# MLP engines bound to source order, and two of four weight-quarter sums made by an accumulating DMA

## The chip, the cores and the metric

One Trainium2 chip, of which this kernel uses one core. The metric is the device time of one execution in microseconds, as the median of several runs. The engines of the core are PE (TensorE, matrix products), DVE (VectorE), ACT (ScalarE), POOL (GpSimd) and SP (SyncE), which here only starts transfers. Each engine runs its own instructions in their order in the program and waits on semaphores for the others.

## What is computed

Two layers of a diffusion backbone over 512 latent tokens and 256 context tokens of width 1024. Each layer has adaLN modulation, an RMSNorm, a token mixer (retention, latent attention, pooling) with a gated residual, then a second norm and the MLP with its gated residual. The change concerns the MLP and what is woven into it:

```python
def rmsnorm(x, g):
    return x * lax.rsqrt(jnp.mean(x * x, axis=-1, keepdims=True) + EPS) * g

def sq_relu_mlp(h, w1, w2):
    return jnp.square(jax.nn.relu(h @ w1)) @ w2

for l in range(DEPTH):
    mod_x = silu(c) @ w_ada[l] + b_ada[l]          # six vectors: sh1, sc1, g1, sh2, sc2, g2
    ...
    x = x + g1 * ox
    x = x + g2 * sq_relu_mlp(modulate(rmsnorm(x, norm_mlp[l]), sh2, sc2), w_ff1[l], w_ff2[l])
    if not last:
        ...
        h = h + cg2 * sq_relu_mlp(modulate(rmsnorm(h, norm_mlp[l]), csh2, csc2), w_ff1[l], w_ff2[l])
return rmsnorm(x, norm_final)
```

Everything is float32. Layer 0 runs the MLP on latent and context tokens, layer 1 on latent tokens alone.

## The kernel before

**Products.** A float32 value is held as a high and a low part; one product of 128 x 128 weights is three matrix multiplications (`mm3`, all of them on line L206). Weights come as raw tiles by DMA and are split by `split_piece`: ACT copies the high part (L214), DVE subtracts it for the low part (L223). The results are the `wt` tiles, six of them.

**The MLP** (`layer_ff`) goes in chunks, eight in layer 0 and four in layer 1. A chunk of layer 0 has four *up* products (tile `f`, from `h`; 48 multiplications of 384 columns each), each evacuated by `evac`: ACT applies ReLU and the square (L1409, L1411), then high and low parts and differences (`T`, L1363, L1364; `act`) are made on ACT and DVE in turn. The first two ups of the first chunk run as one pair (`up_two`), over three groups of tokens, with the norm's last statistics (`ssum`) beside them. Then come two blocks of seven products (A11, S1, A12, S4, S3, S2, A22) of a fast 2 x 2 multiplication scheme, in which two quarters of a weight are first added: S1 = A21 + A22, S3 = A11 + A21, S2 = S1 + A11, S4 = S2 + A12. The four sums are DVE additions (`sum`, L250). A product's PSUM buffer is read out by additions into `V` (L1363) and by *gates*, which add it, scaled, to the residual stream `x` (L1453); there are three such PSUM buffers. The last chunk of each layer is plain: no sums.

**adaLN rows.** While layer 0's MLP runs, the rest of the modulation is computed: some rows as PE products (`ada` from `rows`), the others as dot products on DVE (L474, `dot` and `rows`), one or two for a row. Each row's weights are a 256 KB load (L239) into one of three `rows` tiles. Fourteen such row tasks are merged among the up products of each chunk but the last; the first chunk has eight more, and four ada tasks.

**What sets the order.** `emit` runs the tasks in their order; it loads weight units three ahead on SP's queue (a unit of the blocks is 1 MB, two loads of 512 KB on L231, of four raw tiles in all), splits pieces four ahead, and loads rows up to eight tasks ahead as row tiles become free. A scheduler then reorders each engine's own instructions.

Of the kernel before, what the change touches and what calls it, by code (L numbers as in the profile page):

```python
# [8 lines left out]
F32 = mybir.dt.float32  # L9
F32R = mybir.dt.float32r  # L10
AF = mybir.ActivationFunctionType
ALU = mybir.AluOpType
# [3 lines left out]
P = 128  # L16
# [12 lines left out]
UW = 1024  # L29
# [30 lines left out]
AL = 3  # L60
AU = 4
RA = 8
N_RR = 3
N_DP = 22
N_T = 7
AK = 6
# [10 lines left out]
class Task:  # L77


    def __init__(self, cost, fn, units=()):  # L80
        self.cost, self.fn, self.units = cost, fn, units
# [9 lines left out]
class Unit:  # L91

    def __init__(self, ap, w, kind=None, queue=None):
        self.ap, self.w, self.kind, self.queue = ap, w, kind, queue
        self.raw, self.sums = None, {}
        if kind == "st":
            n = 8  # L100
        elif kind is None:
            n = 1 if w <= OW else -(-w // 512)
        else:
            n = 1
        self.size = w if n == 1 else 512
        self.pieces = [Piece(self, i) for i in range(n)]
        self.nr = {None: 1, "st": 2}.get(kind, 0)
# [19 lines left out]
A11, A12, A22, A21, S1, S2, S3, S4 = range(8)  # L127
# [16 lines left out]
        out.append(t)  # L144


class Net:
    def __init__(self, nc, tc, es, a):
        self.nc, self.tc, self.a = nc, tc, a
        self.n = 0  # L150
        pool = lambda name, bufs, **k: es.enter_context(tc.tile_pool(name=name, bufs=bufs, **k))
        self.cst = pool("cst", 1)
        self.sm = pool("sm", 4)
        self.wr = pool("wr", N_R)
        self.wh = pool("wh", N_W)
        self.tp = pool("tp", N_T)
        self.dp = pool("dp", N_DP)
        self.ps = self.half = None
        self.es = es
        self.psum(3, 2)  # L160
        self.raw, self.hl, self.used = {}, {}, {}
# [64 lines left out]
    def load_unit(self, u):  # L226
        q = u.queue(self.nc) if u.queue else self.nc.sync
        if u.kind == "st":
            u.raw = [self.wr.tile([P, UW], F32, tag="r", name=self.nm("raw")) for _ in range(2)]
            for i in range(2):  # L230
                q.dma_start(u.raw[i], u.ap[:, i * 1024:i * 1024 + 1024])  # L231
            return
        if u.kind == "dp":
            r = self.dp.tile([P, UW], F32, tag="d", name=self.nm("raw"))
        elif u.kind == "wr":
            r = self.wr.tile([P, RW], F32, tag="rr", name=self.nm("rows"), bufs=N_RR)
        else:
            r = self.wr.tile([P, UW], F32, tag="r", name=self.nm("raw"))
        q.dma_start(r[:, :u.w], u.ap)  # L239
        u.raw = r  # L240

    def quarter(self, u, i):

        if i < 4:
            return u.raw[i // 2][:, i % 2 * 512:i % 2 * 512 + 512]
        if i not in u.sums:
            a, b = {S1: (A21, A22), S2: (S1, A11), S3: (A11, A21), S4: (S2, A12)}[i]
            a, b = self.quarter(u, a), self.quarter(u, b)
            t = u.sums[i] = self.tmp("sum")[:, 0:512]
            self.nc.vector.tensor_tensor(t, a, b, op=ALU.add)  # L250
        return u.sums[i]
# [12 lines left out]
    def emit(self, tasks):  # L264
# [37 lines left out]
        for i, t in enumerate(tasks):  # L302
            while ahead < len(rows) and first[rows[ahead]] <= i + RA and sum(end[v] >= i for v in rows[max(0, ahead - 8):ahead]) < N_RR:
                self.load_unit(rows[ahead].unit)
# [1013 lines left out]
    def layer_ff(self, l, whole, groups):  # L1318
# [5 lines left out]
        nc, a = self.nc, self.a  # L1324
        last = l == DEPTH - 1
        w = NL if last else T
# [3 lines left out]
        n_chunk, n_blk = 16 // CP, 4 // MP  # L1330
        halves = [[(0, 256, 0)], [(256, 256, 0)]] if last else [[(0, 384, 0)], [(384, 128, 0), (512, 256, 1)]]
        H = lambda k: self.h[k]
        out = []
# [15 lines left out]
            self.mark = self.lo(lo, src, hi)  # L1349

        def begin():
            n = per * 2 // 4
            t = [self.d("V", F32).rearrange("p a t -> p (a t)") for _ in range(-(-3 // n))]
            for i, name in enumerate("U57"):
                st[name] = [t[i // n][:, (i % n * 4 + j) * hw:(i % n * 4 + j + 1) * hw] for j in range(4)]
                st[name, "all"] = t[i // n][:, i % n * 4 * hw:(i % n + 1) * 4 * hw].rearrange("p (j t) -> p j t", t=hw)
# [75 lines left out]
        def up_two(us):  # L1432

            ps = [self.A("f1") for _ in us]
            for o, n, _ in groups:
                for k in range(NK):
                    s = slice(k * P, (k + 1) * P)
                    for i, u in enumerate(us):
                        self.mm3(ps[i][:, o:o + n], u[:, 0, s], u[:, 1, s],
                                 H(k)[:, 0, o:o + n], H(k)[:, 1, o:o + n], k == 0, k == NK - 1)  # L1440
            for i in range(2):
                for half in range(2):
                    o = half * hw
                    evac(0, i, half, [(ps[i][:, o:o + hw], o, hw)])
# [47 lines left out]
        def finish(j):  # L1492

            U, v5, v7 = (st[n][j] for n in "U57")
            add(v7, v7, U)
            gate(2 * j + 1, 0, v7, True)
            add(U, U, v5)
            add(v7, v7, v5)
            gate(2 * j, 1, U)
            gate(2 * j + 1, 1, v7, True)  # L1500
# [24 lines left out]
        for c in range(n_chunk):  # L1525
            us = [Unit(a["w_ff1"][l, 2 * CP * c + m], 1024) for m in range(2 * CP)]
            m0, ups = 0, []
            cost = self.lin_cost(NK, [(0, hw)] * 2)
            if c == 0:
                m0 = 2  # L1530
                ups.append(Task(0, begin))
                ups.append(Task(2 * cost, lambda us=us: up_two(us[:2]), tuple(us[:2])))
            for m in range(m0, 2 * CP):
                ups.append(Task(cost, lambda c=c, m=m, u=us[m]: up(c, m, u), (us[m],)))
            if c == 0:
                ups.append(Task(0, negate))
            if c == n_chunk - 1:
                ups = merge(ups, [Task(1, lambda j=j: finish(j)) for j in range(4)])
            extra = self.extra.pop(("ff1", l), []) if c == 0 else []
            share = -(-len(spread) // max(n_chunk - 1 - c, 1))  # L1540
            extra, spread = extra + spread[:share], spread[share:]
            out += merge(ups, extra)
            blocks = [Unit(a["w_ff2"][l, c * n_blk + blk], 2048, "st") for blk in range(n_blk)]
            if c < n_chunk - 1:
                for blk in range(n_blk):
                    out += block(c, blk, blocks[blk])
        out.append(Task(0, self.stat_start))
        for blk in range(n_blk - 1):
            out += plain_tasks(c, blocks[blk], blk, whole)
        late = []  # L1550
# [80 lines left out]
def _quarters(w, pairs):  # L1631


    n = 4 // pairs
    t = w.reshape(16 // n, n, 2, P, 4 // pairs, pairs, 2, P)
    t = t.transpose(0, 4, 3, 6, 2, 5, 1, 7).reshape(16, P, 2, 2, 512)
    return np.stack([t[:, :, 0, 0], t[:, :, 0, 1], t[:, :, 1, 1], t[:, :, 1, 0]], axis=2).reshape(16, P, 2048)


def _rope_tables(length, dim):  # L1640
# [101 lines left out]
```

## Time and profile before

| | |
|---|---|
| median of 3 runs | 1658.19 us (1657.01 to 1659.78) |
| the profiled execution | 1657.6 us, its span 1655.8 us |
| PE busy | 1552.9 us, 94% of the span |
| DVE busy | 1183.5 us, 71% |
| ACT busy | 802.4 us, 48% |
| POOL busy | 38.2 us, 2% |
| chain that ended last | PE 84%, DVE 10%, DMA 3%, ACT 3% |

The span is the time from the first to the last instruction of the profiled execution. The chain that ended last is followed back from the last instruction to whatever released each step; it names the engine that sets the end. The idle time shown beside a group of instructions is that of its engine just before them, with the instruction or transfer that ended it.

### The profile page before, as it was taken

The numbers are of one execution on the slowest core, as the hardware profiler recorded it, in microseconds if no ns is written. First come the engines' busy times: TensorE is split into PE (matmuls) and PEld (weight loads), VectorE is DVE, ScalarE is ACT, GpSimd is POOL, SyncE is SP. The second block draws the span as 40 slices with busy tenths as digits, with TensorE's granted clock in tenths as the row PEclk, the third lists the DMA queues.
The fourth block names the chain that finished last, engine by engine and source line by source line (L and its number), as shares of the span: only waits on it lengthen the run. The fifth ranks groups of instructions, "written<-read, shape, count | busy, mean of one in ns | idle before, by whom it ended". The sixth has DMA issues, their size and how long they took to land.

```text
span 1655.8 us, 24510 instructions
## 1 busy us (share of the span) xinstructions
PE 1552.9 (94%) x9100; PEld 1351.4 (82%) x9100; DVE 1183.5 (71%) x2564; ACT 802.4 (48%) x1635; POOL 38.2 (2%) x78
## 2 busy tenths in 40 slices
PE   5999999999869898999999998998999999999997
PEld 2898577878659798899988997976888788888976
DVE  5665756877787979779787948678556785867834
ACT  4425477545334343434434345267764655445443
POOL 0010000000000000000000000101000000000000
PEclk8999999999879899999999999999999999999999
DMA  9352545652433234332432231723433223242321
GB/s 368 112 150 64 148 103 127 193 188 84 128 114 109 96 108 133 116 121 96 131 112 84 88 109 63 208 80 86 101 103 121 77 89 103 71 121 73 119 89 51
DMA packets 69095, 191.98 MB, mean 116 GB/s; under 512 B 8944, under 2 KB 11504, under 8 KB 68976
## 3 DMA queue, kind: packets, MB, share of 16 engines
q1 hardware_dynamic: 65584, 180.18, 34.7%
q0 software_dynamic: 2816, 9.70, 2.6%
q8 instruction: 72, 1.18, 0.3%
q10 hardware_dynamic: 576, 0.52, 0.1%
q14 instruction: 47, 0.39, 0.1%
HBM read 159.97 MB, written 10.49 MB: 103 GB/s over the span
## 4 chain that ended last, share of the span: by engine, by line
PE 84%; DVE 10%; DMA 3%; ACT 3%; issue 1%; SPq 0%; DVEq 0%; ACTq 0%
PE f L206 48%; PE A L206 10%; PE sc L206 4%; PE oe L206 3%; PE pv L206 3%; PE res L206 3%; PE rv L206 2%; PE pT L1031 2%; PE ada L206 2%; DVE act L223 1%; DVE rows L474 1%; PE ro L206 1%; DMA rows<-w_adaT 1%; PE q L206 1%; DVE dot L474 1%; DMA raw<-w_ada 1%
## 5 line engine op out<-in xcount | busy, mean ns | idle before, releaser
L206 PE MATMUL f<-h,wt 128*128 128x384 f32 (+2 forms) x2400 | 466.9, 355 | 10.3 <-ACT b L1409 7.7
L206 PE MATMUL f<-act,wt 128*128 128x256 f32 (+2 forms) x2664 | 436.1, 324 | 41.2 <-DVE x L1453 15.3
L206 PEld LDWEIGHTS f<-h,wt 128*128 128x128 f32 x2400 | 419.9, 191 | 54.3 <-ACT b L1409 14.2
L206 PEld LDWEIGHTS f<-act,wt 128*128 128x128 f32 x2664 | 411.5, 195 | 64.1 <-DVE x L1453 17.2
L223 DVE TENSOR_TENSOR wt<-raw,wt 128x512 fp32r<-128x512 f32 x326 | 222.0, 687 | 150.5 <-ACT wt L214 148.1
L214 ACT ACTIVATE wt<-raw 128x512 fp32r<-128x512 f32 x326 | 201.4, 627 | 228.1 <-PE f L206 124.9
L206 PE MATMUL A<-h,wt 128*128 128x512 f32 (+2 forms) x864 | 171.9, 357 | 1.0 <-ACT h L554 0.5
L206 PEld LDWEIGHTS A<-h,wt 128*128 128x128 f32 x864 | 143.0, 190 | 27.5 <-ACT h L554 2.8
L214 ACT ACTIVATE wt<-sum 128x512 fp32r<-128x512 f32 x104 | 63.0, 628 | 154.2 <-DVE sum L250 143.0
L1409 ACT ACTIVATE b<-f 128x384 f32<-128x384 f32 (+2 forms) x98 | 50.5, 518 | 149.5 <-PE f L206 135.0
L206 PE MATMUL sc<-k,q 96*128 96x512 f32 (+1 forms) x384 | 85.5, 350 | 2.6 <-ACT p L1013 1.9
L474 DVE SCALAR_TENSOR_TENSOR rows<-rows,sbc 128x512 f32<-128x512 f32 x128 | 84.4, 686 | 1.9 <-DMA rows<-w_adaT 1.4
L206 PEld LDWEIGHTS sc<-k,q 96*128 96x128 f32 x384 | 62.8, 188 | 20.4 <-issue 5.5
L1363 DVE TENSOR_TENSOR V<-V,f 128x768 f32<-128x768 f32 (+1 forms) x86 | 62.5, 726 | 21.6 <-PE f L206 21.4
L223 DVE TENSOR_TENSOR wt<-sum,wt 128x512 fp32r<-128x512 f32 x104 | 70.6, 686 | 7.5 <-ACT wt L214 7.3
L1453 DVE SCALAR_TENSOR_TENSOR x<-f,mod,x 128x256 f32<-128x256 f32 (+2 forms) x148 | 68.9, 503 | 6.5 <-PE f L206 4.7
L1012 DVE TENSOR_REDUCE st<-sc 128x1 f32<-128x768 f32 x64 | 60.7, 953 | 15.1 <-PE sc L206 14.7
L1032 ACT ACTIVATE pT<-pT 128x384 f32<-128x384 f32 x128 | 56.5, 491 | 22.4 <-PE pT L1031 22.0
L214 ACT ACTIVATE act<-T 128x384 fp32r<-128x384 f32 (+1 forms) x104 | 47.6, 472 | 38.9 <-DVE T L1364 19.5
L223 DVE TENSOR_TENSOR act<-b,act 128x384 fp32r<-128x384 f32 (+2 forms) x94 | 47.5, 515 | 25.0 <-ACT act L214 24.9
L206 PE MATMUL res<-mix,wt 128*128 128x256 f32 (+1 forms) x384 | 59.1, 313 | 2.3 <-DVE om L1052 1.9
L1013 ACT ACTIVATE p<-sc,st 128x768 f32<-128x768 f32 x64 | 57.8, 905 | 5.6 <-DVE st L1012 4.4
(244 smaller groups left out, 1849.6 us busy)
## 6 DMA issues: line engine op xcount, KB each, us to landing
raw<-w_ff SPq DMA_DIRECT2D x128, 512.0 KB, 3.6
rows<-w_adaT SPq DMA_DIRECT2D x128, 256.0 KB, 3.0
raw<-w_in SPq DMA_DIRECT2D x22, 512.0 KB, 4.1
raw<-w_ada SPq DMA_DIRECT2D x16, 512.0 KB, 10.9
rows<-w_ada SPq DMA_DIRECT2D x32, 256.0 KB, 3.1
raw<-w_out SPq DMA_DIRECT2D x16, 512.0 KB, 3.7
x<-xd SPq DMA_DIRECT2D x6, 768.0 KB, 6.8
x<-xT SPq DMA_DIRECT2D x4, 768.0 KB, 6.5
```

Of the source, the lines that this page charges most:

```text
L206: self.nc.tensor.matmul(out, l, r, start=start, stop=stop)
L214: self.nc.scalar.activation(out, src, AF.Copy, **k)
L223: return self.nc.vector.tensor_tensor(out, src, hi.bitcast(F32), op=ALU.subtract)
L474: nc.vector.scalar_tensor_tensor(out, w, 1.0, self.sbc[:, v, half], op0=ALU.mult, op1=ALU.mult, accum_out=acc[:, v, i, j:j + 1])
L1012: nc.vector.tensor_reduce(st[:, 0:1], ps, axis=AX, op=ALU.max, negate=True)
L1013: nc.scalar.activation(p, ps, AF.Exp, bias=st[:, 0:1], accum_out=st[:, 1:2])
L1031: nc.tensor.transpose(ps[:, kt, :], p[:, (k0 + kt) * P:(k0 + kt + 1) * P], self.ident)
L1032: nc.scalar.activation(s["pT", h, qt // 2][:, k0:k0 + 3, c], ps, AF.Copy)
L1363: add = lambda x, y, z, op=ALU.add: nc.vector.tensor_tensor(x, y, z, op=op)
L1409: nc.scalar.activation(b[:, at:at + n], ps, AF.Relu)
L1453: self.mark = nc.vector.scalar_tensor_tensor(x, ps[:, at - o:at - o + n], g[:, cond:cond + 1], x, op0=ALU.mult, op1=ALU.add)
```

## The change

1. Every instruction that PE, DVE and ACT get between `begin` (ahead of the first up) and `end` (behind the last up of the last chunk) is bound behind the one before it on the same engine, by two wrappers (`Ordered`, `Engines`). The scheduler can no longer reorder them. Transfers are not bound. In the listings below these instructions have the wrapper's line, L164.
2. The quarters of a weight of the blocks are stored as A21, A22, A11, A12. A unit's first raw tile (`sums`) is loaded with A21 twice (L265), the second with A11 and A12 (L266), a third of half the size with A22 (L267), of which there are two. Then GpSimd issues a DMA that adds A22 and A11 to the `sums` tile (L269), which makes it S1 and S3. DVE still adds S2 and S4. The plain chunk's units load A21 without the accumulation.
3. The `rows` tiles become two of three, and the memory set aside for GpSimd's transfers becomes 2048 of 4096.

```diff
-N_RR = 3
+N_RR = 2
...
+class Ordered:
...
+    def __getattr__(self, name):
+        f = getattr(self.engine, name)
+        if name == "dma_start":
+            return f
+        if not self.net.strict:
+            self.last = None
+            return f
+
+        def call(*args, **kw):
+            with self.net.tc.issue_after(self.last.ins) if self.last else nullcontext():
+                self.last = f(*args, **kw)
+            return self.last
+
+        return call
...
-            u.raw = [self.wr.tile([P, UW], F32, tag="r", name=self.nm("raw")) for _ in range(2)]
-            for i in range(2):
-                q.dma_start(u.raw[i], u.ap[:, i * 1024:i * 1024 + 1024])
+            u.raw = [self.wr.tile([P, UW], F32, tag="r", name=self.nm(n)) for n in ("sums", "raw")]
+            u.raw.append(self.wr.tile([P, 512], F32, tag="rh", name=self.nm("raw"), bufs=2))
+            r = u.raw[0].rearrange("p (a c) -> p a c", a=2)
+            if u.plain:
+                q.dma_start(r[:, 0, :], u.ap[:, 0:512])
+            else:
+                q.dma_start(r, u.ap[:, None, 0:512].to_broadcast([P, 2, 512]))
+            q.dma_start(u.raw[1], u.ap[:, 1024:2048])
+            q.dma_start(u.raw[2], u.ap[:, 512:1024])
+            if not u.plain:
+                self.nc.gpsimd.dma_start(u.raw[0], u.ap[:, 512:1536], accum_op=ALU.add)
...
-        if i < 4:
-            return u.raw[i // 2][:, i % 2 * 512:i % 2 * 512 + 512]
+        if i not in (S2, S4):
+            t, o = {A21: (0, 0), S1: (0, 0), S3: (0, 1), A11: (1, 0), A12: (1, 1), A22: (2, 0)}[i]
+            return u.raw[t][:, o * 512:o * 512 + 512]
         if i not in u.sums:
-            a, b = {S1: (A21, A22), S2: (S1, A11), S3: (A11, A21), S4: (S2, A12)}[i]
+            a, b = {S2: (S1, A11), S4: (S2, A12)}[i]
...
         def begin():
+            self.strict = True
...
+        def end():
+            self.strict = False
+            self.stat_start()
+
+        out.append(Task(0, end))
...
-    nc = _bacc.Bacc("TRN2", target_bir_lowering=False, num_devices=1, dynamic_dma_scratch_size=4096)
+    nc = _bacc.Bacc("TRN2", target_bir_lowering=False, num_devices=1, dynamic_dma_scratch_size=2048)
```

PE at the start of layer 0's MLP, before: `res` is the mixer's last projection, `f_846` and `f_847` the first two ups, `ssum` a norm statistic, `ada` the modulation's rows.

```order
L206 MATMUL res_4221<-mix_3386,wt_3861 128x256 x3
L206 MATMUL res_4221<-mix_3768,wt_3861 128x256 x3
L206 MATMUL f_846_4342<-h_763_4024,wt_3932 128x256 x3
L206 MATMUL f_846_4342<-h_764_4025,wt_3932 128x256 x3
L206 MATMUL f_846_4342<-h_765_4026,wt_3932 128x256 x3
...
L206 MATMUL f_846_4342<-h_763_4024,wt_3932 128x256 x3
L206 MATMUL ssum_4245<-ss_3787,one 128x256
L206 MATMUL ada_4303<-rows_4266,sc 32x512
L206 MATMUL ada_4303<-rows_4268,sc 32x512
L206 MATMUL f_847_4343<-h_763_4024,wt_4178 128x256 x3
```

The same place after.

```order
L236 MATMUL res_4224<-mix_3768,wt_3861 128x256 x3
L236 MATMUL ssum_4248<-ss_3787,one 128x256
L164 MATMUL ada_4304<-rows_4269,sc 32x512
L236 MATMUL ssum_4248<-sq_4238,one 128x256
L164 MATMUL ada_4304<-rows_4302,sc 32x512
L164 MATMUL ada_4304<-rows_4314,sc 32x512
L164 MATMUL ada_4304<-rows_4319,sc 32x512
L164 MATMUL f_846_4343<-h_763_4024,wt_3932 128x256 x3
L164 MATMUL f_847_4344<-h_763_4024,wt_4178 128x256 x3
```

The first pair of ups moved from ahead of the last `ssum` to behind it and behind four `ada` products, of which before two stand among the ups.

DVE in a late chunk of layer 0, before, around the evacuation of the second up (`b`, `T`, `act`): the `rows` instructions are dot products, `wt` the low part of a weight.

```order
L474 SCALAR_TENSOR_TENSOR rows_7596,acc_7665<-rows_7596,sbc 128x512
L223 TENSOR_TENSOR act_7713<-b_7710,act_7713 128x384
L223 TENSOR_TENSOR wt_7765<-raw_7570,wt_7765 128x512
L1363 TENSOR_TENSOR T_7742<-b_7710,b_7629 128x384
L1364 SCALAR_TENSOR_TENSOR T_7661<-T_7661,b_7710 128x384
L223 TENSOR_TENSOR act_7713<-b_7710,act_7713 128x384
L223 TENSOR_TENSOR act_7746<-T_7742,act_7746 128x384
L223 TENSOR_TENSOR act_7746<-T_7661,act_7746 128x384
L1364 SCALAR_TENSOR_TENSOR T_7742<-T_7661,b_7710 128x384
L250 TENSOR_TENSOR sum_7768<-raw_7571 128x512
L223 TENSOR_TENSOR act_7753<-T_7742,act_7753 128x384
L474 SCALAR_TENSOR_TENSOR rows_7667,acc_7665<-rows_7667,sbc 128x512
```

The same place after.

```order
L164 TENSOR_TENSOR wt_7669<-raw_7522,wt_7669 128x512
L164 TENSOR_TENSOR act_7707<-b_7704,act_7707 128x384 x2
L164 TENSOR_TENSOR T_7736<-b_7704,b_7620 128x384
L164 TENSOR_TENSOR act_7740<-T_7736,act_7740 128x384
L164 SCALAR_TENSOR_TENSOR T_7652<-T_7652,b_7704 128x384
L164 TENSOR_TENSOR act_7740<-T_7652,act_7740 128x384
L164 SCALAR_TENSOR_TENSOR T_7736<-T_7652,b_7704 128x384
L164 TENSOR_TENSOR act_7747<-T_7736,act_7747 128x384
L164 SCALAR_TENSOR_TENSOR rows_7661,acc_7656<-rows_7661,sbc 128x512
L164 SCALAR_TENSOR_TENSOR rows_7664,acc_7656<-rows_7664,sbc 128x512
L164 SCALAR_TENSOR_TENSOR rows_7751,acc_7656<-rows_7751,sbc 128x512
L164 TENSOR_TENSOR wt_7759<-raw_7559,wt_7759 128x512
```

The evacuation is in one piece now, `T` and `act` in turn, with the split of the next weight and the dots behind all of it; the sum S1 is gone.

SP, the loads of the first chunk's rows, before, with the engines that each load waits for.

```order
L239 DMA rows_4301<-w_adaT 128x512 [waits DMAHW2_49,PE_49]
L239 DMA rows_4306<-w_adaT 128x512 [waits DMAHW3_49,PE_49]
L231 DMA raw_4528<-w_ff 128x1024 [waits DMAHW4_49,DVE_49,Activation_49]
L239 DMA rows_4308<-w_ada 128x512 [waits DMAHW5_49,DVE_49]
L239 DMA rows_4313<-w_ada 128x512 [waits DMAHW6_49,DVE_49]
L239 DMA rows_4318<-w_adaT 128x512 [waits DMAHW7_49,DMAHW5_49,PE_49]
L239 DMA rows_4322<-w_adaT 128x512 [waits DMAHW0_49,DVE_49]
L231 DMA raw_4529<-w_ff 128x1024 [waits DMAHW1_49,DVE_49,Activation_49]
```

The same place after.

```order
L277 DMA rows_4302<-w_ada 128x512 [waits DMAHW3_49,PE_49]
L277 DMA rows_4307<-w_adaT 128x512 [waits DMAHW4_49,DMAHW3_49,PE_49]
L277 DMA rows_4309<-w_adaT 128x512 [waits DMAHW5_49,DVE_49]
L277 DMA rows_4314<-w_ada 128x512 [waits DMAHW6_49,DVE_49]
L277 DMA rows_4319<-w_ada 128x512 [waits DMAHW7_49,DVE_49]
L277 DMA rows_4323<-w_adaT 128x512 [waits DMAHW6_49,DMAHW0_49,PE_49]
L277 DMA rows_4325<-w_adaT 128x512 [waits DMAHW7_49,DMAHW1_49,PE_49]
```

With two tiles, each load from the third on waits for PE's product or DVE's dots on an earlier row, alternately.

## Rows read from the trace of the kernel before

**Rows 1.** The page, part 1: busy us of each engine, its share of the span.

```profile
PE 1552.9 (94%) x9100; PEld 1351.4 (82%) x9100; DVE 1183.5 (71%) x2564; ACT 802.4 (48%) x1635; POOL 38.2 (2%) x78
```

**Rows 2.** Busy time by window: span, then PE, PEld, DVE, ACT, POOL, clock, DMA.

```profile
405.40:512.00 106.60, 86.49 (x437) 73.55 (x438) 85.95 (x214) 40.80 (x82) 0.00 (x0) 0.86 0.37 115
512.00:587.90 75.90, 68.02 (x362) 65.01 (x361) 63.51 (x145) 27.74 (x52) 0.00 (x0) 0.93 0.32 102
...
657.20:726.10 68.90, 65.05 (x361) 64.32 (x361) 54.85 (x114) 28.21 (x52) 0.00 (x0) 0.98 0.37 116
...
1376.90:1466.10 89.20, 87.64 (x531) 77.45 (x530) 65.07 (x136) 44.94 (x88) 0.00 (x0) 0.98 0.33 96
```

**Rows 3.** Timeline of PE, start of layer 0's MLP (start, us, instruction, [idle before]).

```profile
405.39 6.25 PE L206 MATMUL f<-h,wt 128*128 128x256 f32 x51 [0.16 <-DVE x L1243]
...
414.15 13.95 PE L206 MATMUL f<-h,wt 128*128 128x256 f32 x103
428.03 1.04 PE L206 MATMUL ada<-rows,sc 128*32 128x512 f32 x2
```

**Rows 4.** Timeline of PE, the fourth chunk of layer 0.

```profile
657.20 29.91 PE L206 MATMUL f<-h,wt 128*128 128x384 f32 x168
...
688.89 4.40 PE L206 MATMUL f<-h,wt 128*128 128x384 f32 x24
693.13 4.58 PE L206 MATMUL f<-act,wt 128*128 128x384 f32 x25
701.56 24.72 PE L206 MATMUL f<-act,wt 128*128 128x384 f32 x132 [3.85 <-DVE x L1453]
```

**Rows 5.** Timeline of DVE, the same chunk, before and at the gates.

```profile
693.51 0.95 DVE L1363 TENSOR_TENSOR V<-V,f 128x768 f32<-128x768 f32 x1 [2.45 <-PE f L206]
...
697.32 0.69 DVE L250 TENSOR_TENSOR sum<-raw,raw 128x512 f32<-128x512 f32 x1
697.92 0.56 DVE L223 TENSOR_TENSOR act<-T,act 128x384 fp32r<-128x384 f32 x1
...
700.29 0.62 DVE L1453 SCALAR_TENSOR_TENSOR x<-f,mod,x 128x384 f32<-128x384 f32 x1
```

**Rows 6.** Timeline of DVE at the start of layer 0's MLP.

```profile
425.49 0.69 DVE L474 SCALAR_TENSOR_TENSOR dot<-rows,sbc 128x512 f32<-128x512 f32 x1
...
432.19 0.69 DVE L474 SCALAR_TENSOR_TENSOR dot<-rows,sbc 128x512 f32<-128x512 f32 x1 [2.36 <-DMA rows<-w_adaT]
...
434.32 0.69 DVE L474 SCALAR_TENSOR_TENSOR rows<-rows,sbc 128x512 f32<-128x512 f32 x1
```

**Rows 7.** DMA issues: count, KB each, median us to landing.

```profile
raw<-w_ff SPq DMA_DIRECT2D x128, 512.0 KB, 3.6
rows<-w_adaT SPq DMA_DIRECT2D x128, 256.0 KB, 3.0
...
rows<-w_ada SPq DMA_DIRECT2D x32, 256.0 KB, 3.1
...
QQ<-rope POOLq DMA_DIRECT2D x8, 192.0 KB, 7.0
```

**Rows 8.** Timeline of PE, the end of chunk 0 of layer 0.

```profile
471.31 6.97 PE L206 MATMUL f<-h,wt 128*128 128x384 f32 x24 [7.03 <-ACT b L1409]
...
488.21 23.92 PE L206 MATMUL f<-act,wt 128*128 128x384 f32 x120 [3.42 <-ACT wt L214]
```

**Rows 9.** Groups of DVE by line and shape: busy us, mean ns | idle before, releaser.

```profile
L474 DVE SCALAR_TENSOR_TENSOR rows<-rows,sbc 128x512 f32<-128x512 f32 x128 | 84.4, 686 | 1.9 <-DMA rows<-w_adaT 1.4
...
L474 DVE SCALAR_TENSOR_TENSOR dot<-rows,sbc 128x512 f32<-128x512 f32 x64 | 43.0, 685 | 4.4 <-DMA rows<-w_adaT 4.3
...
L250 DVE TENSOR_TENSOR sum<-raw 128x512 f32<-128x512 f32 x26 | 17.8, 685 | 0.0
L250 DVE TENSOR_TENSOR sum<-raw,raw 128x512 f32<-128x512 f32 x26 | 17.8, 684 | 0.0
```

**Rows 10.** Timeline of PE, the first chunk of layer 1.

```profile
1336.38 38.50 PE L206 MATMUL f<-act,wt 128*128 128x256 f32 x300 [2.10 <-ACT wt L214]
```

More of the change, by code (lines that the diff above doesn't have):

```diff
@@ L96, in __init__ @@
     def __init__(self, ap, w, kind=None, queue=None):
-        self.ap, self.w, self.kind, self.queue = ap, w, kind, queue
+        self.ap, self.w, self.kind, self.queue, self.plain = ap, w, kind, queue, False
         self.raw, self.sums = None, {}
@@ L144, in merge, with __init__ @@
         out.append(t)
+class Ordered:
+    def __init__(self, net, engine):
+        self.net, self.engine, self.last = net, engine, None
+    def __getattr__(self, name):
[10 more added lines that the diff above has]
+        return call
+class Engines:
+    def __init__(self, net, nc):
+        self.sync, self.gpsimd = nc.sync, nc.gpsimd
+        self.vector, self.scalar, self.tensor = (Ordered(net, e) for e in (nc.vector, nc.scalar, nc.tensor))
 class Net:
     def __init__(self, nc, tc, es, a):
-        self.nc, self.tc, self.a = nc, tc, a
+        self.strict = False
+        self.nc, self.tc, self.a = Engines(self, nc), tc, a
         self.n = 0
@@ L1543, in layer_ff @@
             blocks = [Unit(a["w_ff2"][l, c * n_blk + blk], 2048, "st") for blk in range(n_blk)]
+            for u in blocks:
+                u.plain = c == n_chunk - 1
             if c < n_chunk - 1:
@@ L1546, in layer_ff @@
                     out += block(c, blk, blocks[blk])
-        out.append(Task(0, self.stat_start))
+        def end():
+            self.strict = False
+            self.stat_start()
+        out.append(Task(0, end))
         for blk in range(n_blk - 1):
@@ L1636, in _quarters @@
     t = t.transpose(0, 4, 3, 6, 2, 5, 1, 7).reshape(16, P, 2, 2, 512)
-    return np.stack([t[:, :, 0, 0], t[:, :, 0, 1], t[:, :, 1, 1], t[:, :, 1, 0]], axis=2).reshape(16, P, 2048)
+    return np.stack([t[:, :, 1, 0], t[:, :, 1, 1], t[:, :, 0, 0], t[:, :, 0, 1]], axis=2).reshape(16, P, 2048)
 def _rope_tables(length, dim):
```

## The prediction, made blind

> **What bounds the kernel now.** I read the page first: PE is busy 1552.9 us of a 1655.8 us span [rows 1], so all that any reordering can win is some 100 us of PE idle time, and all that it can lose is new idle time. Then the stage table [rows 2]. The layer-0 MLP is eight chunks. The first takes 106.6 us with 86.5 us of PE work, the fourth 68.9 us with 65.05 us; a chunk of layer 1 takes 89.2 us with 87.6 us. So waits sit in chunk 0 (20 us), chunk 1 (8 us) and, at 3.85 us a time, in each later chunk of layer 0; layer 1 is nearly full. DVE is the second engine: 86 us busy in chunk 0, 55 in a late chunk.
>
> Then the PE timeline at the two places where the source order will bite. At the start of layer 0's MLP the scheduler lets PE run the first 51 products of f at 405.39, ahead of the last norm sums, and 103 more by 428.03, with the adaLN rows (ada) dropped in behind them [rows 3]. In a late chunk PE runs without a gap until 697.7 and then waits 3.85 us for DVE [rows 4]: the product with S4 needs the PSUM buffer that A11's product holds, and DVE reads that out (the gates, L1453) only from 700.29 until PE goes on at 701.56, because it first evacuates the fourth up product, which ended near 693.5 [rows 4, 5].
>
> **The change part by part.**
>
> *1. Source order at the start of layer 0's MLP.* In the new order PE must run four ada products before the first f, each on a row tile of its own, and there are two row tiles where there were three. The third and fourth ada tiles are loaded only when DVE has read earlier rows with its dots, and DVE reaches those only after the last norm group, near 426.5 (the first dots of before stand among it at 425.49 [rows 6]). So: dots on the first row done 426.7; next row issued, 3.0 us to land [rows 7], 429.8; its two dots 1.4 us (four dots took 432.19 to 435.0 [rows 6]) 431.2; the last ada row issued, 3.1 us [rows 7], 434.4. An ada product is 0.5 to 1.0 us [rows 3]. First f at about 435 instead of 405.4. The 144 products of the first pair of ups then take 144 x 0.125 (51 in 6.25 us, with rounding up [rows 3]) = 18 us and end near 453, against about 425 before (51, 103 and a few between were done by 428.03 [rows 3], so the last dozen belonged to the next up): +28 us, of which nothing is hidden, as no other PE work stands in the program between.
>
> *2. The rest of chunk 0.* The next up product stands behind two more ada products and their transposes. Their rows wait for dots, the dots on DVE stand behind the whole evacuation of the first pair (about 11 us, serial) and two weight splits (0.7 each): dots at 453 + 12.2, then load 3.1, dots 1.4, load 3.1, ada 1.0, transposes about 1.9 makes about 475. Up products 8.4 us each (24 in 4.4 [rows 4], twice): the third and fourth end near 493.5, where before the fourth ended at 478.3 [rows 8]. From there DVE is late: thirteen rows with two dots each are read from two tiles, so a pair of rows costs a load and its own dots, 3.1 + 1.4 = 4.5 us, where it was 2.8. Adding these up along DVE's order, the gates of A11 come near 522, and S4's product with them; before it started at 488.21 [rows 8]. What follows is the same 24 us: chunk 0 ends near 546 instead of 512. **+34.**
>
> *3. Chunks 1 and 2.* Rows have two dots, then partly one. The dots stand in groups of two and three between weight splits and evacuations; the third of a group waits for a load that was issued when its first was read: 3.1 - 1.4 = 1.7 us with two dots, 3.1 - 0.7 = 2.4 with one, three groups a chunk. Before, that wait is 5.7 us in the whole kernel [rows 9]. About **+6** and **+7**.
>
> *4. Chunks 3 to 6.* The same chain, followed from an up product's start at 0: the second ends at 16.8; its evacuation, now strictly ACT, DVE, ACT, DVE, is about 7.2 us (14 operations of about 0.5, against the 5 us from 693.5 to 698.5 of before [rows 5]); three dots with a wait 4.5; two splits 1.3; then the third's evacuation 2.3, three dots with a wait 4.5, a split, two sums and a split 3.4, the fourth's evacuation 7, two dots 1.4, a split 0.7, V 0.95, gates 1.2. That is 51.2, where before it is 701.56 - 657.20 = 44.4 [rows 4]. So S4's wait grows from 3.85 to about 11 us: +7 each, **+28**. Without the row waits it would be +1 to +2.5 each.
>
> *5. Layer 1.* No row work in it. The weights of one up product are split only after the pair's evacuation: one gap of about 3.7 us at the start; the other gaps (2.10 us before the blocks [rows 10]) stay. **+4.**
>
> *6. The sums.* 52 of DVE's 104 additions go: 2 x 17.8 = 35.6 us [rows 9], 2.7 us a chunk of layer 0. DVE has idle time there; what counts is what of it lies before the gates: one sum of 0.69 us at 697.32 inside the chain [rows 5], already left out in step 4. **0**, bounds -0.7 x 7 = -5 and 0.
>
> *7. The accumulating DMAs.* No accumulate is in the trace. Lower bound: a plain 512 KB load, 3.6 us; upper: a load issued by GpSimd of 192 KB takes 7.0 us [rows 7], and scaled by size 512 KB takes 18.7. It starts when the plain load has landed (3.6). In layer 0 the unit is loaded some 18 us or more before S1, so 7 to 22 us is hidden up to 14 us of accumulate. In layer 1 a block is 84 x 0.128 = 10.8 us (300 products in 38.5 us [rows 10]) and two units are in flight: 10.8 to 21.5 us of lead. I take 4 to 8 us, as the row of equal size is the nearest: hidden, **0**; the upper end would put about 4 us on each of 12 units, +48.
>
> *8. The rest.* Two 256 KB loads move to the program's start, ahead of what the first products need; they land in 3.0 us each beside others [rows 7]: 0 to 3 us, **+1**. Longer idles leave PE at the lower clock for a while: after 7.03 us of idle 24 products took 6.97 us [rows 8] where 24 x 0.178 = 4.3 is usual. **+5** over the ten or so longer gaps, bounds 0 and +15.
>
> On step 1's loads the rows say 3.0 and 3.1 us for 256 KB [rows 7]. The Trainium skill ("DMA: Bandwidth & Descriptors", section "Anatomy of one DMA — SWDGE (gpsimd) path") gives a fit of 2.0 us plus bytes over 436e3, an estimate of 2.6 us here; with it each of some 35 load rounds would be about 0.45 us shorter and the sum about 15 us less. The rows are of these very transfers, so they decide.
>
> **Sum**: 34 + 6 + 7 + 28 + 4 + 0 + 0 + 1 + 5 = 85 us on the profiled run's 1657.6, which is the median (1658.2) within 0.6: about **1743 us**.
>
> **The rivals.** *Faster.* DVE is what PE waits for in each layer-0 chunk, and it loses 2.7 us of work there; if the third row of a group has landed when DVE comes to it, and the source order puts the gates earlier than the scheduler did, S4's 3.85 us go seven times (27 us) and layer 1's gaps shrink: about 1635. It decides at whether the gates end before PE has finished the product ahead of S4 (697.7 [rows 4]). Against it: two row tiles instead of three, and the opening, where the new order itself stands PE behind loads. Chance 0.08.
> *Only the opening costs.* If the rows are hidden in the late chunks, steps 1 and 2 (25 to 34), 5, and 1.2 a chunk remain: about 1697. Chance 0.18.
> *Late accumulates.* As in step 7, with ACT's strict order behind each late S1: 85 + 48, about 1790. Chance 0.11.
> *No effect.* The bound order costs nothing because the queues wait in much the same places anyway: 1655 to 1661. The program's order shows the first f behind four ada products, which speaks against it. Chance 0.03.
> The forecast has 0.60.
>
> **How the numbers follow.** A difference of 0.2% is about what this kernel's measurement can tell from none. Slower: 0.60 + 0.18 + 0.11 = 0.89; same 0.03; faster 0.08. The range takes in the forecast with its bounds, the opening alone and the late accumulates at their price: 1688 to 1792, leaving out the faster and equal cases and the outer ends of the others.
>
> **What would show it.** Steps 1 and 2: PE idle from about 408 to 435, put down to DMA of the adaLN rows, and again for some 15 us before the third up product; a wrong step 1 shows f products before 415. Steps 3 and 4: DVE idle <-DMA rows<-w_adaT of about 50 us in all instead of 5.7, and PE's wait before S4 near 11 us with the gates as releaser. Step 5: one gap of 3 to 4 us after layer 1's first pair. Step 6: sum<-raw and sum<-raw,raw gone. Step 7: the accumulates' time to landing; over 14 us the forecast is too low. If the waits before S4 stay at 4 us or less, step 4 is wrong and the time is near 1700.

## The result

The changed kernel took 1902.33 us (1899.92 to 1905.89), the kernel before 1657.6 us beside it: a ratio of 1.1476, 95% interval 1.1454 to 1.1498. It is slower, as forecast, but by 245 us where the forecast said 85; the time lies outside the range. The profiled execution has a span of 1904.1 us, 248.3 more than before.

The page after: busy time [rows 1], the clock by slice, the groups of the up products (whose wait for ACT's `b` was 7.7 us before), of the high parts of sums on ACT, of the dots (the first half of [rows 9]), and of the transfers [rows 7].

```profile
PE 1607.1 (84%) x9100; PEld 1392.4 (73%) x9100; DVE 1172.9 (62%) x2512; ACT 807.0 (42%) x1635; POOL 60.9 (3%) x104
...
PEclk8999999997698989898988998999998899998999
...
L164 PE MATMUL f<-h,wt 128*128 128x384 f32 (+2 forms) x2400 | 499.7, 370 | 117.0 <-ACT b L164 114.1
...
L164 PE MATMUL f<-act,wt 128*128 128x384 f32 (+1 forms) x2184 | 362.8, 328 | 90.8 <-DVE x L164 74.8
...
L164 DVE SCALAR_TENSOR_TENSOR rows<-rows,sbc 128x512 f32<-128x512 f32 x104 | 70.1, 689 | 46.1 <-DMA rows<-w_adaT 44.1
...
L164 ACT ACTIVATE wt<-sum 128x512 fp32r<-128x512 f32 x52 | 32.4, 623 | 143.9 <-DVE sum L164 143.9
...
rows<-w_adaT SPq DMA_DIRECT2D x128, 256.0 KB, 2.8
...
sums<-w_ff POOLq DMA_DIRECT2D x26, 512.0 KB, 6.0
```

PE does the same 9100 multiplications. It waits about 194 us more (1904.1 - 1607.1 = 297 idle, against 103), and the same work takes 54 us longer, at a lower granted clock (0.931 of full speed in this execution, 0.972 before). The up products alone wait 114 us for `b` on ACT, which is ACT's reading of the up product's PSUM buffer. No such wait was in the forecast.

By stage, from PE's timeline. A chunk runs from its first up to the next chunk's; chunk 0 of layer 0 begins at the end of the mixer's last projection, layer 1's first chunk behind the last `ssum` among its ups.

| stage | before, us | after, us | difference | forecast |
|---|---|---|---|---|
| start to the end of the mixer's last projection, layer 0 | 405.4 | 412.7 | +7.3 | +1 |
| layer 0, chunk 0 | 106.6 | 145.9 | +39.4 | +34 |
| chunk 1 | 75.9 | 89.4 | +13.5 | +6 |
| chunk 2 | 69.4 | 89.4 | +20.1 | +7 |
| chunks 3 to 6 | 274.5 | 344.8 | +70.3 | +28 |
| chunk 7 to layer 1's MLP | 351.8 | 356.3 | +4.5 | 0 |
| layer 1, chunks 0 to 2 | 271.4 | 361.3 | +89.9 | +4 |
| the last chunk and the end | 100.9 | 104.4 | +3.4 | 0 |

(+5 of the forecast was for the clock and has no stage.)

**The opening went as forecast.** PE's timeline, which answers to [rows 3] and [rows 8]:

```profile
410.35 2.34 PE L236 MATMUL res<-mix,wt 128*128 128x256 f32 x16
...
437.36 1.92 PE L164 MATMUL ada<-rows,sc 128*32 128x512 f32 x2 [11.36 <-DMA rows<-w_ada]
440.07 1.92 PE L164 MATMUL ada<-rows,sc 128*32 128x512 f32 x2 [0.80 <-DMA rows<-w_ada]
441.92 18.21 PE L164 MATMUL f<-h,wt 128*128 128x256 f32 x144
460.06 1.05 PE L164 MATMUL ada<-rows,sc 128*32 128x512 f32 x4
479.31 2.56 PE L164 MATMUL ada<-rows,sc 128*32 128x512 f32 x4 [18.20 <-DMA rows<-w_ada]
...
515.17 6.15 PE L164 MATMUL f<-h,wt 128*128 128x384 f32 x24 [15.50 <-ACT b L164]
```

The first up begins 29.2 us after the projection's end (forecast 29.6), the third 24.2 us after the pair's end at 460.1 (forecast 22). In the listing of SP's loads after the change the third and fourth `ada` rows (`rows_4314`, `rows_4319`) wait for DVE, as step 1 needs; waits for PE and for DVE do not alternate there. The last line was not forecast: 15.5 us before the *second half* of the fourth up, put down to ACT's reading of its first half.

**A late chunk**, the fourth of layer 0, answering to [rows 4]:

```profile
737.41 4.33 PE L164 MATMUL f<-h,wt 128*128 128x384 f32 x24
742.31 8.59 PE L164 MATMUL f<-h,wt 128*128 128x384 f32 x48 [0.58 <-ACT b L164]
751.49 8.59 PE L164 MATMUL f<-h,wt 128*128 128x384 f32 x48 [0.58 <-ACT b L164]
763.94 10.27 PE L164 MATMUL f<-h,wt 128*128 128x384 f32 x48 [3.86 <-ACT b L164]
779.97 6.81 PE L164 MATMUL f<-h,wt 128*128 128x384 f32 x24 [5.77 <-ACT b L164]
786.62 6.40 PE L164 MATMUL f<-act,wt 128*128 128x384 f32 x36
798.06 25.45 PE L164 MATMUL f<-act,wt 128*128 128x384 f32 x132 [5.04 <-DVE x L164]
```

An up is 48 multiplications, 24 for each half of its tokens. The gaps come after 24, then after every 48: always between the two halves of one up, never between two ups. Each half is written into its own half of one PSUM buffer, and in the program, as in the one before, the second half waits until ACT has read the first: 0.49 us for the instruction, 0.58 us with what lies around it. Before, the scheduler had put multiplications of the next up between the halves, here four. This is the order of PE before, in a chunk of layer 0 (the last row of the first half, then the next up, then the first row of the second half):

```
L206 MATMUL f_1063_5735<-h_770_4031,wt_5666 128x384 x3
L206 MATMUL f_1075_5816<-h_763_4024,wt_5685 128x384 x3
L206 MATMUL f_1075_5816<-h_764_4025,wt_5685 128x384
L206 MATMUL f_1063_5735<-h_763_4024,wt_5646 128x384 x3
```

0.58 us is the least of it. Where ACT comes late to that reading, PE waits for whatever holds ACT. ACT's and DVE's timelines a chunk earlier, before the fourth up's second half began at 694.63:

```profile
682.62 0.62 ACT L164 ACTIVATE wt<-raw 128x512 fp32r<-128x512 f32 x1
693.57 0.63 ACT L164 ACTIVATE wt<-sum 128x512 fp32r<-128x512 f32 x1 [10.34 <-DVE sum L164]
694.11 0.47 ACT L164 ACTIVATE b<-f 128x384 f32<-128x384 f32 x1
```

```profile
686.86 0.69 DVE L164 SCALAR_TENSOR_TENSOR rows<-rows,sbc 128x512 f32<-128x512 f32 x1 [2.34 <-DMA rows<-w_adaT]
...
690.51 0.69 DVE L164 SCALAR_TENSOR_TENSOR rows<-rows,sbc 128x512 f32<-128x512 f32 x1 [2.27 <-DMA rows<-w_adaT]
...
692.13 0.68 DVE L164 TENSOR_TENSOR sum<-sums,raw 128x512 f32<-128x512 f32 x1
692.85 0.69 DVE L164 TENSOR_TENSOR sum<-sum,raw 128x512 f32<-128x512 f32 x1
```

Read from the bottom up: two dots wait for their rows, the sum S4 stands behind them on DVE, the high part of S4 waits for the sum on ACT, the reading of `f` stands behind it on ACT, and the second half of the up waits for that on PE. Late 256 KB loads reach three engines this way, since none may pass its own waiting instruction. The two waits are 4.6 of the 10.34 us that ACT stands still here; the rest is DVE's own work ahead of the sum.

**Layer 1** has no rows, and still lost some 30 us a chunk. There two products of 12 multiplications share a PSUM buffer, one in each half, and the same gap comes after every second product:

```profile
1617.06 1.57 PE L164 MATMUL f<-act,wt 128*128 128x256 f32 x12
1625.06 4.53 PE L164 MATMUL f<-act,wt 128*128 128x256 f32 x24 [6.42 <-DVE x L164]
1630.17 3.09 PE L164 MATMUL f<-act,wt 128*128 128x256 f32 x24 [0.58 <-DVE x L164]
1633.86 3.06 PE L164 MATMUL f<-act,wt 128*128 128x256 f32 x24 [0.60 <-DVE V L164]
1639.31 3.09 PE L164 MATMUL f<-act,wt 128*128 128x256 f32 x24 [2.39 <-DVE x L164]
```

The stage table, a late chunk of layer 0 and the second of layer 1, against [rows 2]:

```profile
737.41:823.35 85.94, 70.11 (x362) 68.52 (x361) 53.33 (x108) 27.82 (x52) 1.75 (x2) 0.90 0.40 111
1563.51:1681.75 118.24, 93.40 (x530) 80.22 (x529) 63.27 (x128) 46.09 (x88) 3.47 (x4) 0.94 0.38 98
```

Of the 17 us in layer 0 some 12 are idle time and 5 the same multiplications at a lower granted clock (0.90 against 0.98); of the 29 in layer 1, 23 and 6. DVE is less busy than before in both.

### The profile page after: what moved, and what is told of

Its sections match the earlier page's. It is cut to its first block, busy times and chain, and to the rows that moved or that the text cites. A ratio compares the mean times of both kernels' runs of the same rounds, so it can differ in the third digit from the quotient of the medians.

```text
span 1904.1 us, 24671 instructions
## 1 busy us (share of the span) xinstructions
PE 1607.1 (84%) x9100; PEld 1392.4 (73%) x9100; DVE 1172.9 (62%) x2512; ACT 807.0 (42%) x1635; POOL 60.9 (3%) x104
## 4 chain that ended last, share of the span: by engine, by line
PE 50%; DVE 12%; ACT 8%; DMA 3%; issue 2%; DVEq 0%; ACTq 0%
PE f L164 32%; PE A L236 4%; PE f L236 4%; ACT b L164 3%; DMA rows<-w_adaT 3%; DVE act L164 3%; ACT act L164 3%; DVE T L164 2%; ACT wt L164 2%; PE sc L236 2%; DVE wt L164 1%; PE oe L236 1%; PE pv L236 1%; DVE sum L164 1%; PE pT L1070 1%
## 5 line engine op out<-in xcount | busy, mean ns | idle before, releaser
L164 PE MATMUL f<-h,wt 128*128 128x384 f32 (+2 forms) x2400 | 499.7, 370 | 117.0 <-ACT b L164 114.1
L164 PEld LDWEIGHTS f<-h,wt 128*128 128x128 f32 x2400 | 446.7, 203 | 168.5 <-ACT b L164 130.0
L164 PE MATMUL f<-act,wt 128*128 128x384 f32 (+1 forms) x2184 | 362.8, 328 | 90.8 <-DVE x L164 74.8
L164 PEld LDWEIGHTS f<-act,wt 128*128 128x128 f32 x2184 | 351.1, 201 | 101.7 <-DVE x L164 65.8
L164 ACT ACTIVATE wt<-raw 128x512 fp32r<-128x512 f32 x204 | 122.8, 623 | 143.4 <-PE f L164 137.2
L164 ACT ACTIVATE b<-f 128x384 f32<-128x384 f32 (+2 forms) x98 | 50.4, 514 | 262.5 <-PE f L164 262.5
L164 DVE TENSOR_TENSOR act<-b,act 128x384 fp32r<-128x384 f32 (+2 forms) x94 | 47.3, 517 | 183.5 <-ACT act L164 183.4
L164 DVE TENSOR_TENSOR wt<-raw,wt 128x512 fp32r<-128x512 f32 x204 | 136.3, 685 | 19.3 <-ACT wt L164 17.4
L244 ACT ACTIVATE wt<-raw 128x512 fp32r<-128x512 f32 (+2 forms) x116 | 72.3, 630 | 115.6 <-PE A L236 36.8
L253 DVE TENSOR_TENSOR wt<-raw,wt 128x512 fp32r<-128x512 f32 (+2 forms) x116 | 78.9, 687 | 58.5 <-ACT wt L244 57.6
L164 DVE SCALAR_TENSOR_TENSOR rows<-rows,sbc 128x512 f32<-128x512 f32 x104 | 70.1, 689 | 46.1 <-DMA rows<-w_adaT 44.1
L164 ACT ACTIVATE wt<-sum 128x512 fp32r<-128x512 f32 x52 | 32.4, 623 | 143.9 <-DVE sum L164 143.9
L164 ACT ACTIVATE act<-T 128x384 fp32r<-128x384 f32 (+1 forms) x104 | 49.4, 475 | 96.8 <-DVE T L164 96.8
L164 DVE TENSOR_TENSOR act<-T,act 128x384 fp32r<-128x384 f32 (+1 forms) x104 | 51.7, 497 | 56.3 <-ACT act L164 56.3
L164 DVE TENSOR_TENSOR V<-V,f 128x768 f32<-128x768 f32 (+1 forms) x86 | 62.6, 728 | 35.9 <-PE f L164 35.6
L164 DVE SCALAR_TENSOR_TENSOR x<-f,mod,x 128x256 f32<-128x256 f32 (+2 forms) x148 | 68.6, 502 | 26.2 <-PE f L164 22.4
L236 PE MATMUL f<-act,wt 128*128 128x256 f32 (+1 forms) x480 | 81.7, 329 | 0.5 <-DVE x L1282 0.5
L236 PEld LDWEIGHTS sc<-k,q 96*128 96x128 f32 x384 | 63.1, 188 | 20.1 <-ACT p L1052 6.0
```

Source lines behind the costliest of these rows:

```text
L164: self.last = f(*args, **kw)
L236: self.nc.tensor.matmul(out, l, r, start=start, stop=stop)
L244: self.nc.scalar.activation(out, src, AF.Copy, **k)
L253: return self.nc.vector.tensor_tensor(out, src, hi.bitcast(F32), op=ALU.subtract)
```

## The experiments

All kernels of one batch were timed beside the kernel before. The bound kernels of the experiments ran once each; runs of one kernel here lie within 13 us of each other. The theory: the source order on the three engines costs the time, through the two halves of a PSUM buffer. The rivals: the row tiles, the accumulating DMA, and lateness of ACT and DVE that has nothing to do with PE's order.

**1. The binding alone.** The kernel before with `Ordered` and `Engines` added; no other part of the change.

```diff
+        self.nc, self.tc, self.a = Engines(self, nc), tc, a
...
         def begin():
+            self.strict = True
```

> The kernel before with only the source-order binding added: the four sums stay on VectorE, three row tiles stay. Theory (the binding is the cause: in source order the second half of a PSUM buffer comes right behind the first, so PE waits for ACT or DVE to read the first half, 0.58 us at best and 4 to 10 us where ACT or DVE is itself held by its order): most of the +246 us is here, 1830 to 1880 us, with layer 1's chunk near 118 us and a gap of about 0.6 us after nearly every second product. Rival (the row tiles and the accumulating DMA are the cause, as the forecast had it in part): under 1750 us, layer 1's chunk near 90 us.

Measured: 1946.7 us (+289). The theory's sign and its pattern of gaps hold, but its numbers were too low (a chunk of layer 1 takes 129.6 us and not 118), since the binding alone costs more than the whole change. So the other parts together give some of it back.

**2. The change without the binding.**

```diff
-            self.strict = True
+            self.strict = False
```

> The changed kernel with the binding taken out; accumulating DMA and two row tiles stay. Theory (binding is the cause): 1655 to 1680 us; the mixer of layer 0 keeps its +7 us from two row tiles, layer 1's chunk is back at 88 to 90 us. Rival (accumulate and row tiles): above 1780 us.

Measured: 1684.2 us, ratio 1.0172 (1.0135 to 1.0209). The binding is worth 218 us in the changed kernel; what remains, +26, is a little above the theory's range. Layer 1's chunks are 97.1, 90.6 and 87.8 us, against 93.5, 89.2 and 88.7 before, so the first is not back.

**3. Two row tiles and nothing else.**

```diff
-N_RR = 3
+N_RR = 2
```

> The kernel before with two row tiles instead of three and nothing else. Theory: +7 us in the mixer and up to 10 us in the first chunks of layer 0's MLP, where rows have two dots each, together 1665 to 1675 us. Rival (the row loads are what the chunks of layer 0 wait for): +40 us or more, 1700 us.

Measured: 1683.3 us, ratio 1.0167 (1.0141 to 1.0193). That is +25, above my range and as much as all of the remaining +26: with two row tiles and without the binding, the accumulating DMA is worth nothing. The starts of the chunks show where: layer 0's first up begins 5 us later (410.8 against 405.4, the mixer's rows), the fourth chunk 24.6 us later (681.8 against 657.2), the eighth 25.8. The rows cost in the mixer and in chunks 0 to 2, where they have two dots or partly two, and next to nothing in late chunks. That the scheduler puts other work ahead of a dot there is a likely reason, not a shown one, and with the accumulating DMA late chunks do pay (experiment 7).

**4. A PSUM buffer for each half.** Bound as the change is; each half of an up, and each product of layer 1, gets one of the three buffers to itself.

```diff
-            ps = self.A("f1", (P, 2, 512))
             for half in range(2):
+                ps = self.A("f1", (P, 2, 512))
...
-        if self.half is None:
-            self.half = self.A(name, (P, 2, 512))
-            return self.half[:, 0, :]
-        t, self.half = self.half, None
-        return t[:, 1, :]
+        return self.A(name, (P, 2, 512))[:, 0, :]
```

> The changed kernel, but each half of an up product of layer 0 and each product of layer 1 gets a PSUM buffer of its own (three buffers as before, one half of each unused), so that no product waits for the reading of the other half. Theory: layer 1's chunk loses its 0.6 us gaps, 118 to about 98 us, each later chunk of layer 0 loses 5 to 10 of its 16 added us, in all about 100 to 130 us less: 1770 to 1800 us. Rival (the gaps come from ACT and DVE being late in their own order, whatever buffer is used): within 20 us of 1902.

Measured: 1766.7 us, 136 less than the change, a little more than the theory said. PE's timeline of it, a late chunk of layer 0 and the second of layer 1:

```profile
797.16 33.44 PE L164 MATMUL f<-h,wt 128*128 128x384 f32 x192
830.44 2.25 PE L164 MATMUL f<-act,wt 128*128 128x384 f32 x12
837.34 6.65 PE L164 MATMUL f<-act,wt 128*128 128x384 f32 x24 [4.65 <-ACT b L164]
849.13 24.65 PE L164 MATMUL f<-act,wt 128*128 128x384 f32 x132 [5.14 <-DVE x L164]
```

```profile
1479.10 45.15 PE L164 MATMUL f<-h,wt 128*128 128x512 f32 x192
1524.08 4.48 PE L164 MATMUL f<-act,wt 128*128 128x256 f32 x36
1533.64 38.02 PE L164 MATMUL f<-act,wt 128*128 128x256 f32 x300 [5.07 <-DVE x L164]
```

All 192 multiplications of the ups run without a gap, and in layer 1 the last 300 multiplications, behind one wait of 5 us, too. Layer 1's chunk is 1571.5 - 1479.1 = 92.4 us, near 89.2 before. The gaps were waits on the other half of a buffer; this is shown, not only argued. Layer 0's chunk is 873.6 - 797.2 = 76.5 us, still 8 above before: PE waits there 4.65 us for ACT's `b` and 5.14 for the gates.

**5. Which engine's order.** Four kernels leave the binding off some engines of the changed kernel; the first of the four edits:

```diff
-        self.vector, self.scalar, self.tensor = (Ordered(net, e) for e in (nc.vector, nc.scalar, nc.tensor))
+        self.vector, self.scalar = (Ordered(net, e) for e in (nc.vector, nc.scalar))
+        self.tensor = nc.tensor
```

> The changed kernel with PE left to the scheduler; DVE and ACT stay bound. Theory (the source order on PE sets the waits on the other half of a PSUM buffer, and the opening behind the adaLN rows): both go, 1902 - 136 - 25 = 1730 to 1770 us. Rival (what costs is that ACT and DVE are late in their own order): 1850 us or more.

> The changed kernel with PE alone bound; DVE and ACT are left to the scheduler. Theory (the waits are on PE's order, and grow from 0.6 to 4 or 10 us only where ACT or DVE is held by its own order): the 0.6 us gaps and the opening stay, the long ones shrink, 1770 to 1810 us. Rival (PE's order alone does it): 1880 us or more; the other rival (only ACT's and DVE's order): under 1700.

> The changed kernel with ACT left to the scheduler; PE and DVE stay bound. PE alone bound took 1766 us, all three 1902. If ACT's order is what holds the reading of PSUM (its read of an up product stands behind the high part of a sum that DVE has not made yet, 10 us at a time), 1780 to 1820 us. If DVE's order is (dots and weight splits ahead of what ACT waits for), 1860 us or more.

> The changed kernel with DVE left to the scheduler; PE and ACT stay bound. If DVE's order is what makes ACT late, 1780 to 1820 us; if ACT's own order is, 1850 us or more.

| bound | us | above none bound |
|---|---|---|
| none | 1684.2 | |
| PE | 1765.6 | 81 |
| PE and ACT | 1796.3 | 112 |
| PE and DVE | 1845.4 | 161 |
| ACT and DVE | 1847.5 | 163 |
| all three | 1902.3 | 218 |

The first expectation was wrong: with PE free, 163 of the 218 us stay. The theory had put too much on PE's order; ACT and DVE in source order are late by themselves, and PE waits for them in the scheduler's order too (57 us for ACT's `b`, 55 for DVE's `x`, 44 for ACT's `wt`). Of the others, the kernel with PE bound alone came out 4 us under its range, the one with ACT free between its two ranges, the one with DVE free inside the first of its two. Between the two engines, DVE's order is the dearer: added to PE's it costs 80 us, ACT's 31. With PE bound alone the 0.58 us gaps stay and the long ones shrink, as expected; a late chunk of layer 0:

```profile
753.83 4.33 PE L164 MATMUL f<-h,wt 128*128 128x384 f32 x24
758.74 8.59 PE L164 MATMUL f<-h,wt 128*128 128x384 f32 x48 [0.58 <-ACT b L1450]
767.91 8.59 PE L164 MATMUL f<-h,wt 128*128 128x384 f32 x48 [0.58 <-ACT b L1450]
779.35 10.16 PE L164 MATMUL f<-h,wt 128*128 128x384 f32 x48 [2.85 <-ACT b L1450]
790.49 4.43 PE L164 MATMUL f<-h,wt 128*128 128x384 f32 x24 [0.98 <-ACT b L1450]
```

Such a chunk takes 71 us (753.8 to 825.0), 2 to 3 more than before, while a chunk of layer 1 takes 112 of the 118 us. So in layer 0 the late readers cost most, in layer 1 PE's order is enough for most of the loss.

**6. The accumulating DMA and the rows under the binding.**

> The kernel before with the binding and two row tiles; the four sums stay on VectorE. It differs from the changed kernel by the accumulating DMA alone. Theory (under the binding, ACT's high part of a sum waits for DVE's addition, 293 us in all with four sums on DVE against 144 with two, and whatever stands behind it on ACT waits too): the accumulating DMA is a gain in this order, so 1950 to 1975 us here against 1902. Rival (the accumulating DMA gains nothing, as without the binding): 1890 to 1915 us.

Measured: 1995.0 us. With two row tiles and the binding, the accumulating DMA is a *gain* of 93 us (1995.0 to 1902.3), more than expected; with three tiles it is 93 us too (1946.7 in experiment 1, 1853.8 below). The view of waits, ACT's high parts of sums; first this kernel, with four sums on DVE:

```profile
ACT wt L163 <- DVE sum L163: 296.8, 73, 15.8
```

and the changed kernel:

```profile
ACT wt L164 <- DVE sum L164: 143.9, 26, 15.8
```

S1 and S3 by DMA have no DVE instruction that ACT's queue has to wait for. That the 93 us come by this wait is argued: ACT waits 143.0 us for sums in the kernel before, too, so what counts is what stands behind the wait, and no run isolates that.

The changed kernel with three row tiles:

```diff
-N_RR = 2
+N_RR = 3
...
-    nc = _bacc.Bacc("TRN2", target_bir_lowering=False, num_devices=1, dynamic_dma_scratch_size=2048)
+    nc = _bacc.Bacc("TRN2", target_bir_lowering=False, num_devices=1, dynamic_dma_scratch_size=512)
```

> The changed kernel with three row tiles (memory for GpSimd's transfers 512 instead of 2048 makes the room); all engines bound. With the sums on DVE the third tile was worth 1995 - 1947 = 48 us under the binding, 25 us without it. Theory (a dot that waits for its row holds everything behind it on DVE, then ACT and PE): 1850 to 1860 us. Rival (the row tiles' price is the same in any order): 1875 to 1880 us.

Measured: 1853.8 us, 48.5 less than with two tiles, as much as with the sums on DVE (1995.0 to 1946.7), and twice the 25 us of experiment 3. The number is in the theory's range, but the 25 us are from kernels with the sums on DVE. Like for like, with the accumulating DMA and without the binding, the third tile is worth 46 us (1684.2 in experiment 2, 1637.9 in experiment 7). The rival with that price would have said 1856 us and fits as well. So that the binding makes a late row dearer is shown with the sums on DVE, and not with the accumulating DMA.

**7. The accumulating DMA without the binding, with three row tiles.**

> The accumulating DMA with three row tiles and no binding (memory for GpSimd's transfers 512 instead of 2048, which makes room for the third tile). Theory (two row tiles cost the 25 us, the accumulating DMA nothing): 1652 to 1664 us, equal to before within 0.4%. Rival (VectorE's 35.6 us are worth time once rows don't wait): 1640 us or less.

Measured: 1637.9 us (1634.1 to 1645.0), ratio 0.9888 (0.9867 to 0.9910). 1.1% faster than before, and on the rival's side: with three row tiles the 26 transfers do buy time, with two they bought none. DVE's waits for rows are 5.2 us here, 34.5 in experiment 3 and 55.3 in experiment 2; that two tiles turn the time that DVE is spared into waiting for rows fits these numbers, and no run isolates it. A late chunk, against [rows 4]:

```profile
674.91 4.32 PE L236 MATMUL f<-h,wt 128*128 128x384 f32 x24
679.07 4.84 PE L236 MATMUL f<-act,wt 128*128 128x384 f32 x27
684.74 2.36 PE L236 MATMUL f<-act,wt 128*128 128x384 f32 x12 [0.82 <-DVE x L1493]
687.97 21.07 PE L236 MATMUL f<-act,wt 128*128 128x384 f32 x120 [0.87 <-DVE V L1403]
```

The 3.85 us before S4 are 1.7 in two pieces, and the 132 multiplications from there on take 23.4 us instead of 24.7; chunks 3 to 6 take 65.2 us each instead of 68.6 (68.4 to 71.6 in experiment 2). In layer 1 the chunks became longer instead, 95.7, 91.8 and 90.5 us against 93.5, 89.2 and 88.7. There the DMA is late once in each chunk: DVE's addition for S2 waits 3.2, 3.8 and 3.3 us for it, and PE then 3.0, 3.5 and 2.9 us for a gate behind that addition. DVE and PE in the second chunk:

```profile
1423.60 0.69 DVE L289 TENSOR_TENSOR sum<-sums,raw 128x512 f32<-128x512 f32 x1 [3.80 <-DMA sums<-w_ff]
```

```profile
1426.66 17.57 PE L236 MATMUL f<-act,wt 128*128 128x256 f32 x132 [3.45 <-DVE x L1493]
```

So the last run keeps the DMA in layer 0 alone:

```diff
+                u.dve = l == DEPTH - 1
```

> Accumulating DMA in layer 0 alone, layer 1's four sums on DVE as before, three row tiles, no binding. In the kernel with it in both layers layer 0's late chunks took 65.3 us against 68.5, layer 1's 91 against 89. Theory (DVE's additions cost time where dots share DVE with them, in layer 0, and a later S1 costs some in layer 1): 1628 to 1634 us. Rival (layer 1's 2 us a chunk come from elsewhere): 1636 to 1642 us.

Measured: 1632.1 us (1627.7 to 1634.0), ratio 0.9849 (0.9830 to 0.9867), with layer 1's chunks at 92.0, 89.4 and 88.7. This is the fastest kernel of the study, 25 us under the kernel before. Why those transfers of layer 1 land late was not taken further.

## Why the prediction was wrong, step by step

*Step 1, 2 (chunk 0, +34).* Right in mechanism and nearly in size: +39.4. The first up, the third up, and DVE's order behind them came as worked out (the row loads, taken at 3.0 and 3.1 us, landed in 2.8 and 3.3); S4's product began at 535.8, which is 528.5 without the 7.3 us of the mixer, against 522. The part that was missing is the 15.5 us before the fourth up's second half, partly beside DVE's own lateness.

*Steps 3 and 4 (chunks 1 to 6, +41).* These failed: +104. The chain was followed along DVE and ACT to the gates alone, and PE was taken to run its ups without a gap. The listing of the order had both facts in it: the second half of each up has a wait for ACT at its first row, and the high part of S4 stands ahead of ACT's reading of the fourth up. I read the first as a wait for the buffer's earlier use, long fulfilled, and used the second only for the gates. S4's own wait was 5 us and not 11, because PE had lost the time already, before S4. That the kernel came out slower, as forecast, is therefore no success of these steps.

*Step 5 (layer 1, +4).* Failed by the most: +90 in three chunks. "No row work in it" was true, and beside the point. Layer 1's products share buffers in pairs, and in source order each pair's second product follows its first directly. Nothing in the rows of before could show this, because the scheduler's interleaving was what hid it; but the trace of before had 300 multiplications in 38.5 us [rows 10] with no gap, and the question "what lies between two writes to one buffer, and what will lie there after" was not asked.

*Step 6 (the sums, 0, lower bound -5).* Mis-sized. Unbound and with three row tiles, the relief of DVE is worth 3.4 us in each late chunk, the mechanism that the faster rival describes; with two tiles it is worth nothing; bound, 93 us.

*Step 7 (accumulate, hidden).* Right for the changed kernel: 6.0 us to land, inside the 4 to 8 taken, and never late enough to show in the waits of PE, ACT or DVE. Unbound it is late in layer 1 (experiment 7).

*Step 8 (the clock, +5, bounds 0 and +15).* Mis-sized: PE's busy time grew by 54 us. The price per gap was about right, 0.5 us forecast and some 0.6 measured; there are not ten such gaps but five in each of chunks 1 to 6 of layer 0 and some eighteen in each of three chunks of layer 1.

*The row tiles* were costed inside the MLP only. The mixer of layer 0 loads rows too: of the +7.3 us by the end of its projection, the kernel with two row tiles alone has +5.4. The forecast of DVE's waits for rows, about 50 us, is 44.1 + 19.0 = 63 us for the two kinds of dots.

The bound of each step was set around the mechanism I had found; none was set for mechanisms that the old order hides. Here that was the larger part.

## What to carry to other kernels

Before an order is fixed, list for each engine what stands between the two uses of every shared buffer in the scheduler's order, and what will stand there in source order: a wait of half a microsecond that was always covered appears once for every buffer. In a fixed order the price of a late load is not its own lateness but everything queued behind it on each engine in turn. A change made of several parts should be run in its parts, and in more than one combination: here one part gained 18 to 25 us with three row tiles and was buried under one that lost 218; and two row tiles cost 25 us unbound and 48 bound where DVE makes all the sums, but 46 unbound and 48 bound where DMA makes two of them.

## What was not expected of the hardware

- An accumulating DMA of 512 KB lands in 6.0 us (median of 26) in the bound kernel and 7.4 us in the unbound one with the same row tiles, against 3.6 us for a plain load of the same size on SP's queue. With the memory for GpSimd's transfers at 512 instead of 2048 (and three row tiles) it was 7.3 us, so that size made no visible difference here.
- The same 9100 multiplications took 54 us more of PE's busy time: 24 of them 6.81 us after a wait of 5.77, where 4.33 is usual, and 48 of them 10.27 after 3.86 us, where 8.59 is. The granted clock of these stretches is 0.62 and 0.83 of full speed, so for part of each it was the lower of its two levels (1.2 GHz); it is 1.00 (2.4 GHz) in the 48 after a wait of 0.58 us.
